# Differential attention in a four-layer trunk: where the heads' splits, the last projection and the first value weights stand in the order of work

## The chip, the cores and the metric

The kernel runs on one core of a Trainium2 chip. The core has five engines, each with its own in-order queue: TensorE (PE in the profile, with its weight loads shown apart as PEld), VectorE (DVE), ScalarE (ACT), GpSimd (POOL) and SyncE (SP), which here only issues loads. The metric is the device time of one execution in microseconds, as the median of several runs. Lower is better.

## The reference

A trunk of four layers over a sequence of 512 positions with 1024 channels, in float32. Layers 0 and 3 mix by a state space (S5), layer 1 by gated linear attention, layer 2 by differential attention; each mixer is followed by a gated feed-forward block. The change touches layer 2's mixer alone:

```python
q, k, v = jnp.split(h @ w_qkv, 3, axis=-1)
q = partial_rope(q.reshape(bsz, seq, 2 * DIFF_HEADS, DIFF_HD), positions) * DIFF_HD ** -0.5
k = partial_rope(k.reshape(bsz, seq, 2 * DIFF_HEADS, DIFF_HD), positions)
v = v.astype(f32).reshape(bsz, seq, DIFF_HEADS, 2 * DIFF_HD)
lam = exp(sum(lam_q1 * lam_k1)) - exp(sum(lam_q2 * lam_k2)) + lambda_init
...
s = jnp.einsum('bqhd,bkhd->bhqk', qb, k)                      # per block of 128 queries
mask = chunk_id[:, None, None, :] <= qcid[:, None, :, None]   # chunks of 64 positions
p = jax.nn.softmax(jnp.where(mask, s, NEG_INF), axis=-1)
a = p[:, :, 0] - lam * p[:, :, 1]
o = jnp.einsum('bhqk,bkhd->bqhd', a, v)
...
o = o * lax.rsqrt(jnp.mean(o * o, axis=-1, keepdims=True) + 1e-5) * subln_g * (1.0 - lambda_init)
x = x + o.reshape(bsz, seq, D_MODEL) @ w_o
```

There are eight heads, each with two score maps of 64 dimensions and values of 128 dimensions.

## The kernel before, in words

**Products.** A float32 product is made of three faster ones. Each operand is split into a high half, a rounded copy made by ACT, and a low half, the difference, made by DVE; `mm3` (L394, matmuls L396 to L398) adds high x high, high x low and low x high into one PSUM accumulator. Weights come in blocks of 256 rows by 512 columns: `wb` (L388) loads a block on SP into one of three staging buffers `wst` (L357) and splits it (L368 on ACT, L376 on DVE) into one of five buffers `whl`.

**Units.** `gemm_units` (L440) is a generator over a projection of 512 output columns: one unit is one `mm3`, for one k tile of 128 rows and one of the four position tiles t, and a projection has 32 units. It asks for a block's load and split just before that block's first unit. At the last k tile each t's accumulator is given to an evacuation function at once.

**Order of the queues.** In this layer the order on PE is the program's own, written by hand. On ACT, DVE, POOL and SP a scheduler that simulates the engines chooses: the ready instruction that comes first in the program goes first, so an instruction can be pulled far ahead of its place when the simulated engine is free, and a queue then runs in the order so fixed. `tc.issue_after(ins)` keeps the instructions made inside it behind `ins` in the order of that engine's queue; it adds no semaphore.

**The layer.** Projections come in the order `project(hf, z)`, half of the heads `hf`, `z` = 0, 1, 2 for q, k, v: the three of half 0, then three of half 1. For q and k the evacuation scales (ACT, L2197) and rotates (DVE, L2202 to L2208) the result, and a `turn` (four PE transposes L2213, one ACT copy L2214 into `qk`) is put into a queue that is due six units later. For v it is one ACT instruction into `vall` (L2219).

`prepare(j)` (L2228) makes head j's operands ready: the split of its q and k (`hl`, ACT L2233, DVE L2234) and eight DMAs on POOL that spread the halves into `qs` (two buffers) and `ks` (in the `whl` buffers). `hl` has one buffer, except for head 1.

The loop has 32 passes, called steps here; step i serves head j = i // 4 and query tile t = i % 4. Its order on PE: `turned(i)`, four transposes of the weighted map `pr` (L2281; ACT copies them to `aT`, L2283); `scores(i + 2)`, four matmuls (L2259) whose softmax (row minimum on DVE L2263, exponential on ACT L2267, combination on DVE L2274) has two steps to finish; `done`, once per head, four transposes of the normalised output (L2314) and its split into `oT` (L516 on ACT, L517 on DVE); some units; `values(i)`, the matmuls with the values (L2291), whose result ACT copies (L2294) and squares (`junk`, L2296); more units. `prepare(j + 1)` stands in the first step of head j. All these transposes and the values share two PSUM banks (`tp`), the scores have two, the projections four.

The units of steps 0 to 14 are those of half 1's projections (`units`, of which ten run ahead of the loop); from step 16 on they are the output projection's first half (`last`), one before and one after the values. The output projection's second half follows the loop with weight blocks `w1` that are asked for at steps 26 and 29. After the layer the feed-forward block runs in a written-out order on all engines.

Of the kernel before, what the change touches and what calls it, by code (L numbers as in the profile page):

```python
# [11 lines left out]
F32 = mybir.dt.float32  # L12
# [3 lines left out]
AF = mybir.ActivationFunctionType  # L16
ALU = mybir.AluOpType
# [5 lines left out]
D = 1024  # L23
SEQ = 512
NT = SEQ // P
KT = D // P
# [262 lines left out]
class Trunk:  # L289
# [147 lines left out]
                    )  # L437
                evac(t, accs[t])

    def gemm_units(self, stat, w, nk, c0, evac):  # L440

        accs = [self.acc() for _ in range(NT)]
        for kb in range(0, nk, 2):
            hl = self.wb(w, kb, c0)
            if kb == 2:
                self.flush()
            for a in range(2):
                k = kb + a
                for t in range(NT):
                    self.mm3(  # L450
                        accs[t][:], stat(k, 0, t), stat(k, 1, t), hl[:, 0, a], hl[:, 1, a], k == 0, k == nk - 1,
                    )
                    if k == nk - 1:
                        evac(t, accs[t])
                    yield
# [1675 lines left out]
    def diff(self, l, left):  # L2131
# [4 lines left out]
        with self.tc.tile_pool(name="diff", bufs=1) as p:  # L2136
# [36 lines left out]
            nc.gpsimd.dma_start(xdv, self.x[:])  # L2173
            vall = []

            queue, clock = [], [0]

            def run(units, n=None):

# [12 lines left out]
            def project(hf, z):  # L2192
                qk = qks[hf]

                def evac(t, ps):
                    q = self.np_.tile([P, 512], F32, tag=("h", "hh")[t % 2], name="qtm", bufs=2)
                    nc.scalar.mul(q[:], ps[:], r[:, t : t + 1])  # L2197
                    s3 = ps[:].rearrange("p (h d) -> p h d", d=64)
                    q3 = q[:].rearrange("p (h d) -> p h d", d=64)
                    ro = p.tile([P, 2, 8, 16], F32, tag="ro", name="ro", bufs=2)  # L2200
                    c2 = cos2[:, t].unsqueeze(1).broadcast_to([P, 8, 16])
                    v.tensor_tensor(ro[:, 0], s3[:, :, 0:16], c2, op=ALU.mult)  # L2202
                    for y in range(2):
                        s1 = sin2[:, t, y * 8 : y * 8 + 8].unsqueeze(1).broadcast_to([P, 8, 8])
                        v.tensor_tensor(  # L2205
                            ro[:, 1, :, y * 8 : y * 8 + 8], s3[:, :, 8 - 8 * y : 16 - 8 * y], s1, op=ALU.mult
                        )
                    v.tensor_tensor(q3[:, :, 0:16], ro[:, 0], ro[:, 1], op=ALU.add)  # L2208

                    def turn():  # L2210
                        tp = self.tp("qTp")
                        for j in range(4):
                            nc.tensor.transpose(tp[:, j], q[:, j * P : (j + 1) * P], self.ident[:])  # L2213
                        nc.scalar.copy(qk[:, z, :, t * P : (t + 1) * P], tp[:])  # L2214

                    queue.append((clock[0] + 6, turn))

                def evac_v(t, ps):
                    nc.scalar.mul(vall[0][:, t, hf * 512 : (hf + 1) * 512], ps[:], r[:, t : t + 1])  # L2219

                if z == 2 and not vall:
                    vall.append(self.xp.tile([P, NT, D], F32, tag="x", name="vall"))
                yield from self.gemm_units(stat, w, KT, z * D + hf * 512, evac_v if z == 2 else evac)

            ready, kept = {}, {}

            def prepare(j):


                room, bufs, tag = (self.wp, 5, "whl") if j == 1 else (p, 1, "hl")  # L2230
                hl = room.tile([P, 2, 2, SEQ], F32R, tag=tag, name="hl", bufs=bufs)
                src = qks[j // 4][:, :, j % 4]
                nc.scalar.copy(hl[:, 0], src)  # L2233
                v.tensor_tensor(hl[:, 1], src, hl[:, 0].bitcast(F32), op=ALU.subtract)  # L2234
                qs = p.tile([P, 2, SEQ], F32R, tag="qs", name="qs", bufs=2)
                ks = self.wp.tile([P, 2, 2, SEQ], F32R, tag="whl", name="ks", bufs=5)
                for m in range(2):
                    rows = slice(m * 64, (m + 1) * 64)
                    for z in range(2):
                        to = slice(z * 64, (z + 1) * 64)  # L2240
                        self.nc.gpsimd.dma_start(qs[to, m], hl[rows, z, 0])
                        self.nc.gpsimd.dma_start(ks[to, m], hl[rows, :, 1])
                ready[j] = qs, ks
                st = self.sp.tile([P, 2, NT], F32, tag="st", name="st", bufs=4)
                o_s = p.tile([P, NT, P], F32, tag="o_s", name="o_s", bufs=2)
                kept[j] = st, o_s
# [3 lines left out]
            def scores(i):  # L2250
                j, t = divmod(i, NT)
                ts = slice(t * P, (t + 1) * P)
                qs, ks = ready[j]
                st = kept[j][0]
                pr, sums = [], self.sp.tile([P, 4], F32, tag="sums", name="sums", bufs=4)
                ss = [self.sbank("s"), self.sbank("s")]
                for m in range(2):
                    for z in range(2):
                        nc.tensor.matmul(ss[m][:], qs[:, m, ts], ks[:, m, z], start=z == 0, stop=z == 1)  # L2259
                for m in range(2):  # L2260
                    e = T("pr", 4)
                    nm = self.sp.tile([P, 1], F32, tag="nm", name="nm", bufs=4)
                    v.tensor_tensor_reduce(  # L2263
                        e[:], ss[m][:], mask[:, t], -0.125, 3e38, op0=ALU.add, op1=ALU.min, accum_out=nm[:]
                    )
                    sum_ = st[:, 0, t : t + 1] if m == 0 else sums[:, 1:2]
                    nc.scalar.activation(e[:], e[:], AF.Exp, scale=-1.0, bias=nm[:], accum_out=sum_)  # L2267
                    pr.append(e)
                v.reciprocal(sums[:, 2:3], sums[:, 1:2])
                v.tensor_scalar(  # L2270
                    sums[:, 3:4], st[:, 0, t : t + 1], sums[:, 2:3], self.neglam[:], op0=ALU.mult, op1=ALU.mult
                )
                a = pr[0]
                v.scalar_tensor_tensor(a[:], pr[1][:], sums[:, 3:4], pr[0][:], op0=ALU.mult, op1=ALU.add)  # L2274
                soft[i] = a
# [24 lines left out]
            def normalised(j):  # L2300
                st, o_s = kept.pop(j)
                q2 = self.sp.tile([P, NT], F32, tag="q2", name="q2", bufs=2)
                v.tensor_tensor(q2[:], st[:, 0], st[:, 0], op=ALU.mult)
                v.scalar_tensor_tensor(q2[:], q2[:], 1e-5, st[:, 1], op0=ALU.mult, op1=ALU.add)
                rs = self.rsqrt(q2[:], NT, 0.0)
                for t in range(NT):
                    v.scalar_tensor_tensor(
                        o_s[:, t], o_s[:, t], rs[:, t : t + 1], sg[:], op0=ALU.mult, op1=ALU.mult
                    )

                def done():
                    tp = self.tp("oTp")
                    for t in range(NT):
                        nc.tensor.transpose(tp[:, t], o_s[:, t], self.ident[:])  # L2314
                    if j == 4:
                        oT[1] = p.tile([P, 2, 4, SEQ], F32, tag="qk", name="oT1", bufs=2)[:].bitcast(F32R)
                    o = oT[j // 4]
                    self.split_t(o[:, 0, j % 4], o[:, 1, j % 4], tp[:].rearrange("p a b -> p (a b)"))

                return done  # L2320

# [33 lines left out]
            run(units, 2)  # L2355
            for i in range(32):
                j, t = divmod(i, NT)
                if i == 15:
                    run(units)
                    rest()  # L2360
                src, n = (units, (3, 3)) if i < 15 else (last, (1, 1))
                if i in (15, 28, 31):
                    n = (0, 0)
                elif i == 29:
                    n = (0, 2)
                aT = turned(i)
                if t == 0 and j < 7:
                    prepare(j + 1)
                if i < 30:
                    scores(i + 2)  # L2370
                if i in done:
                    done.pop(i)()
                run(src, n[0])
                values(i, aT)
                run(src, n[1])
                if i in (16, 31):
                    back(i // 31)
                if i in (26, 29):
                    w1 += [self.wb(wo, kb, 512) for kb in ((0, 2) if i == 26 else (4, 6))]
                if t == 3:  # L2380
                    done[i + (2 if j in (6, 7) else 3)] = normalised(j)
            self.x = vall[0]
# [95 lines left out]
```

## Time and profile before

| | |
|---|---|
| median of three runs | 2300.09 us (2299.6 to 2303.49) |
| the profiled execution | 2300.71 us, span of the core 2298.6 us |
| mean granted TensorE clock | 0.987 |
| instructions | 37231 |
| attention layer, first projection's units to the last output units | about 1166 to 1455 us of the span |
| the loop's 32 groups of four transposes (L2281) | 1248.2 to 1417.2 us |

How to read the rows: a timeline row gives start, length, engine, line, operation, output <- input, and in brackets how long the engine idled before it and what ended that. "PE busy" counts modelled ends, so PE can wait a little less than PEld does. A row of a stretch gives the stretch, its length, the busy time of PE, PEld, DVE, ACT and POOL with their numbers of instructions in brackets, the granted clock, the DMA share and GB/s.

### The profile page before, as it was taken

The numbers are of one execution on the slowest core, as the hardware profiler recorded it, in microseconds if no ns is written. First come the engines' busy times: TensorE is split into PE (matmuls) and PEld (weight loads), VectorE is DVE, ScalarE is ACT, GpSimd is POOL, SyncE is SP. The second block draws the span as 40 slices with busy tenths as digits, with TensorE's granted clock in tenths as the row PEclk, the third lists the DMA queues.
The fourth block names the chain that finished last, engine by engine and source line by source line (L and its number), as shares of the span: only waits on it lengthen the run. The fifth ranks groups of instructions, "written<-read, shape, count | busy, mean of one in ns | idle before, by whom it ended". The sixth has DMA issues, their size and how long they took to land. (4 is left out here: it accounts for less than half of the span.)

```text
span 2298.6 us, 37231 instructions
## 1 busy us (share of the span) xinstructions
PE 2212.9 (96%) x14847; PEld 1961.5 (85%) x14847; DVE 1566.1 (68%) x2430; ACT 1119.9 (49%) x1865; POOL 280.4 (12%) x386
## 2 busy tenths in 40 slices
PE   5889999999999999999999999999999899999997
PEld 3778979898877799998987787989999788989996
DVE  8873887776624469777744675886766964967674
ACT  5534645454452456555535675754534224635342
POOL 1000140512000010101002131110000100101000
PEclk8899999999999999999999999999999999999999
DMA  4136566664422357666336465886641546666521
GB/s 87 39 111 188 139 180 169 171 173 109 121 69 79 123 134 203 183 166 171 98 116 144 95 141 150 214 229 147 163 104 47 143 144 163 176 173 168 159 78 64
DMA packets 295319, 317.83 MB, mean 138 GB/s; under 512 B 72205, under 2 KB 235337, under 8 KB 294890
## 3 DMA queue, kind: packets, MB, share of 16 engines
q1 hardware_dynamic: 232906, 234.23, 33.3%
q0 software_dynamic: 62240, 81.22, 18.9%
q8 instruction: 117, 1.92, 0.3%
q14 instruction: 56, 0.46, 0.1%
HBM read 283.54 MB, written 16.65 MB: 131 GB/s over the span
## 5 line engine op out<-in xcount | busy, mean ns | idle before, releaser
L376 DVE TENSOR_TENSOR whl<-wst,whl 128x1024 fp32r<-128x1024 f32 x272 | 331.1, 1222 | 254.8 <-ACT whl L368 254.2
L368 ACT CAST whl<-wst 128x1024 fp32r<-128x1024 f32 x272 | 284.0, 1050 | 314.7 <-PE acc L398 223.6
L563 PE MATMUL a<-side,whl 128*128 128x256 f32 x3168 | 382.4, 277 | 3.9 <-DVE whl L376 3.6
L563 PEld LDWEIGHTS a<-side,whl 128*128 128x128 f32 x3168 | 369.1, 188 | 6.7 <-DVE whl L376 5.4
L396 PE MATMUL acc<-whl,act 128*128 128x512 f32 x704 | 278.4, 396 | 1.4 <-DVE x L546 1.4
L397 PE MATMUL acc<-whl,act 128*128 128x512 f32 x704 | 274.8, 390 | 0.0
L398 PE MATMUL acc<-whl,act 128*128 128x512 f32 x704 | 274.7, 390 | 0.0
L563 PE MATMUL c<-side,whl 128*128 128x256 f32 x2112 | 254.5, 277 | 1.2 <-DVE whl L376 1.2
L563 PEld LDWEIGHTS c<-side,whl 128*128 128x128 f32 x2112 | 246.8, 188 | 2.0 <-DVE whl L376 2.0
L376 DVE TENSOR_TENSOR whl<-slot,whl 128x1024 fp32r<-128x1024 f32 x107 | 130.4, 1221 | 69.9 <-ACT whl L368 69.9
L396 PEld LDWEIGHTS acc<-whl,act 128*128 128x128 f32 x704 | 132.2, 188 | 31.7 <-issue 2.5
L398 PEld LDWEIGHTS acc<-whl,act 128*128 128x128 f32 x704 | 132.2, 188 | 28.1
L397 PEld LDWEIGHTS acc<-whl,act 128*128 128x128 f32 x704 | 132.2, 188 | 25.6
L368 ACT CAST whl<-slot 128x1024 fp32r<-128x1024 f32 x107 | 112.2, 1053 | 82.3 <-PE acc L398 34.9
L396 PE MATMUL acc<-whl,hT 128*128 128x512 f32 x352 | 144.0, 409 | 2.1 <-DVE ro L2205 1.5
L397 PE MATMUL acc<-whl,hT 128*128 128x512 f32 x352 | 138.9, 395 | 0.9 <-DVE whl L376 0.9
L398 PE MATMUL acc<-whl,hT 128*128 128x512 f32 x352 | 139.2, 395 | 0.0
L563 PE MATMUL a<-sides,whl 128*128 128x256 f32 x1056 | 134.5, 283 | 0.0
L563 PEld LDWEIGHTS a<-sides,whl 128*128 128x128 f32 x1056 | 129.7, 191 | 1.2
L563 PE MATMUL d<-sides,whl 128*128 128x256 f32 x1056 | 126.5, 276 | 1.0 <-ACT whl L368 1.0
L563 PEld LDWEIGHTS d<-sides,whl 128*128 128x128 f32 x1056 | 122.8, 188 | 1.2 <-ACT whl L368 1.2
L702 ACT CAST act<-r 128x512 fp32r<-128x512 f32 (+1 forms) x110 | 66.4, 646 | 114.4 <-DVE r L681 107.3
(452 smaller groups left out, 3891.5 us busy)
## 6 DMA issues: line engine op xcount, KB each, us to landing
wst<-in_ffn_w_gate_up_dram SPq DMA_DIRECT2D x88, 512.0 KB, 4.9
wst<-in_ffn_w_down_dram SPq DMA_DIRECT2D x88, 512.0 KB, 4.1
slot<-in_ffn_w_gate_up_dram SPq DMA_DIRECT2D x71, 512.0 KB, 5.6
wst<-in_ffn_w_gate_up_dram POOLq DMA_DIRECT2D x44, 512.0 KB, 6.0
halves<-in_ffn_w_gate_up_dram SPq DMA_DIRECT2D x43, 512.0 KB, 5.5
wst<-in_s_w_glu_dram SPq DMA_DIRECT2D x32, 512.0 KB, 4.4
wst<-in_gla_w_in_dram SPq DMA_DIRECT2D x24, 512.0 KB, 3.6
wst<-in_diff_w_qkv_dram SPq DMA_DIRECT2D x24, 512.0 KB, 4.0
```

What stands on the lines that cost most here:

```text
L368: self.last["high"] = self.nc.scalar.copy(hl[:, 0], w[:])
L376: self.last["low"] = self.nc.vector.tensor_tensor(hl[:, 1], w[:], hl[:, 0].bitcast(F32), op=ALU.subtract)
L396: mm(out, lh, rh, start=first, stop=False)
L397: mm(out, lh, rl, start=False, stop=False)
L398: self.last["mm"] = mm(out, ll, rh, start=False, stop=last)
L563: mm(o, hl[:, x, k, c], side[y][:, k], start=first and not (j or k or n), stop=k == 3 and n == 2, skip_group_check=True,)
L702: self.last["act high"] = nc.scalar.copy(dst[:, 0, j], src[:, j])
```

## The change

Six edits, all in the layer's order of work; no computation is added or removed.

- `gemm_units` gets `early`: with it, each block's load and split is asked for before the units of the block ahead of it. Only the value projection of half 0 uses it.
- The turns of half 1's q projection are due 6 + t units after their evacuation, so two units apart.
- `prepare(j)`'s ACT copy is tied behind the last evacuation into `vall` made so far (j below 3; none exists yet for j = 0), or behind the last exponential of `scores(4j - 5)` (j from 3).
- Units: at step 3 four units run before the scores and two after the values; steps 9 to 11 take five, steps 12 to 14 four, and step 15 the rest.
- `done` stands at the head of its step, for steps before 29.
- `w1`'s first block is asked for at step 24, the second at 26, and the splits of the two asked for at step 29 are tied behind the copy into `oT`.

```diff
-    def gemm_units(self, stat, w, nk, c0, evac):
+    def gemm_units(self, stat, w, nk, c0, evac, early=False):
         accs = [self.acc() for _ in range(NT)]
+        nxt = None
         for kb in range(0, nk, 2):
-            hl = self.wb(w, kb, c0)
+            hl = nxt or self.wb(w, kb, c0)
+            nxt = self.wb(w, kb + 2, c0) if early and kb + 2 < nk else None
...
-            queue, clock = [], [0]
+            queue, clock, behind = [], [0], {}
...
-                    queue.append((clock[0] + 6, turn))
+                    queue.append((clock[0] + 6 + (t if hf > z else 0), turn))

                 def evac_v(t, ps):
-                    nc.scalar.mul(vall[0][:, t, hf * 512 : (hf + 1) * 512], ps[:], r[:, t : t + 1])
+                    behind["vall"] = nc.scalar.mul(vall[0][:, t, hf * 512 : (hf + 1) * 512], ps[:], r[:, t : t + 1])
...
-                yield from self.gemm_units(stat, w, KT, z * D + hf * 512, evac_v if z == 2 else evac)
+                yield from self.gemm_units(
+                    stat, w, KT, z * D + hf * 512, evac_v if z == 2 else evac, early=z == 2 and not hf
+                )
...
             def prepare(j):
+                tie = behind.get("vall" if j < 3 else 4 * j - 7)
...
-                nc.scalar.copy(hl[:, 0], src)
+                with self.tc.issue_after(tie.ins) if tie else nullcontext():
+                    nc.scalar.copy(hl[:, 0], src)
...
-                    nc.scalar.activation(e[:], e[:], AF.Exp, scale=-1.0, bias=nm[:], accum_out=sum_)
+                    behind[i - 2] = nc.scalar.activation(
+                        e[:], e[:], AF.Exp, scale=-1.0, bias=nm[:], accum_out=sum_
+                    )
...
-                    self.split_t(o[:, 0, j % 4], o[:, 1, j % 4], tp[:].rearrange("p a b -> p (a b)"))
+                    hi = o[:, 0, j % 4]
+                    src = tp[:].rearrange("p a b -> p (a b)")
+                    behind["oT"] = nc.scalar.copy(hi, src)
+                    v.tensor_tensor(o[:, 1, j % 4], src, hi.bitcast(F32), op=ALU.subtract)
...
-                if i == 15:
+                if i == 16:
                     run(units)
                     rest()
-                src, n = (units, (3, 3)) if i < 15 else (last, (1, 1))
-                if i in (15, 28, 31):
+                src, n = (units, (3, 3)) if i < 16 else (last, (1, 1))
+                if i in (28, 31):
                     n = (0, 0)
                 elif i == 29:
                     n = (0, 2)
+                elif 9 <= i < 12:
+                    n = (3, 2)
+                elif 12 <= i < 15:
+                    n = (2, 2)
+                if i in done and i < 29:
+                    done.pop(i)()
                 aT = turned(i)
                 if t == 0 and j < 7:
                     prepare(j + 1)
+                if i == 3:
+                    run(src, 4)
+                    n = (0, 2)
                 if i < 30:
                     scores(i + 2)
                 if i in done:
...
-                if i in (26, 29):
-                    w1 += [self.wb(wo, kb, 512) for kb in ((0, 2) if i == 26 else (4, 6))]
+                for kb in {24: (0,), 26: (2,), 29: (4, 6)}.get(i, ()):
+                    self.behind = {"silu": behind["oT"], "scaled": behind["oT"]} if i == 29 else None
+                    w1.append(self.wb(wo, kb, 512))
+                    self.behind = None
```

`self.behind` is what `high` and `low` (L365, L371) read to put a split behind the named instructions.

## Prediction

> **What bounds the kernel now.** I read the page's busy shares first, then a table of stretches through the attention layer, then what the weight loads (PEld) wait for there, and last the timeline around each of those waits.
>
> ```profile
> PE 2212.9 (96%) x14847; PEld 1961.5 (85%) x14847; DVE 1566.1 (68%) x2430; ACT 1119.9 (49%) x1865; POOL 280.4 (12%) x386
> ```
>
> TensorE bounds the whole, at 96%. No edit changes the matmuls, so only PE's idle time inside this layer can be won. Stretches of the layer (length, then busy PE, PEld, DVE, ACT and POOL with instruction counts, clock, DMA):
>
> ```profile
> 1170.00:1240.00 70.00, 68.44 (x312) 56.01 (x310) 24.77 (x56) 24.55 (x33) 6.89 (x12) 0.98 0.49 137
> 1270.00:1290.00 20.00, 17.18 (x98) 13.94 (x97) 13.02 (x42) 14.01 (x32) 4.34 (x5) 1.00 0.14 38
> 1320.00:1350.00 30.00, 29.98 (x166) 25.36 (x164) 18.34 (x46) 18.77 (x46) 10.06 (x17) 1.00 0.66 141
> 1350.00:1380.00 30.00, 27.89 (x169) 23.56 (x170) 26.11 (x71) 24.80 (x70) 12.23 (x19) 1.00 0.63 134
> 1380.00:1421.00 41.00, 35.38 (x206) 27.88 (x205) 27.52 (x75) 26.15 (x77) 4.13 (x4) 1.00 0.37 96
> 1421.00:1455.00 34.00, 34.00 (x197) 29.44 (x197) 16.94 (x24) 20.92 (x57) 5.74 (x5) 1.00 0.85 209
> ```
>
> PE idles at four places: before 1240 (1.6 us, with a clock below 1), at 1270 to 1290 (2.8), and 2.1 and 5.6 us in the two stretches from 1350 on, where softmaxes run with few projection units between them. Around these PE is full. What PEld waited for between 1170 and 1421 (total us, times, longest):
>
> ```profile
> PEld op L2291 <- ACT aT L2283: 5.5, 7, 1.5
> PEld acc L396 <- ACT oT L516: 2.8, 2, 1.9
> PEld acc L396 <- ACT qtm L2197: 1.9, 1, 1.9
> PEld acc L398 <- DVE oT L517: 1.4, 2, 1.0
> PEld op L2291 <- ACT qk L2214: 1.4, 1, 1.4
> PEld oTp L2314 <- ACT junk L2296: 1.4, 2, 1.1
> PEld acc L397 <- DVE whl L376: 1.3, 1, 1.3
> PEld aTp L2281 <- DVE oT L517: 1.2, 1, 1.2
> PEld acc L396 <- ACT whl L368: 1.1, 1, 1.1
> PEld s L2259 <- DVE nm L2263: 1.0, 2, 0.6
> PEld aTp L2281 <- ACT junk L2296: 0.7, 1, 0.7
> ```
>
> These are 19.7 us, nearly all on copies made by ACT and DVE, not on DMA or PE. PEld counts also the gap that PE's pipeline covers, so I take a little less than each row.
>
> **Part 1: the value projection's weights a step ahead.**
>
> ```profile
> 1218.42 1.05 ACT L2233 CAST hl<-qk 128x1024 fp32r<-128x1024 f32 x1
> 1219.38 2.93 ACT L368 CAST whl<-wst 128x1024 fp32r<-128x1024 f32 x3
> 1220.47 0.19 PEld L396 LDWEIGHTS acc<-whl,hT 128*128 128x128 f32 x1 [1.05 <-ACT whl L368]
> 1221.92 0.19 PEld L397 LDWEIGHTS acc<-whl,hT 128*128 128x128 f32 x1 [1.26 <-DVE whl L376]
> 1219.47:1222.89 3.42, 1.86 (x7) 1.04 (x6) 3.38 (x3) 2.84 (x4) 2.75 (x5) 1.00 0.54 104
> 1222.89:1226.30 3.41, 3.41 (x9) 2.66 (x9) 1.25 (x2) 0.00 (x0) 1.80 (x4) 0.50 1.00 230
> ```
>
> The second weight block of the value projection is split only after head 0's split, because the program asks for it after `prepare(0)`. PE waits 1.05 us for its high half and 1.26 for its low half. In the next 3.41 us the clock is 0.50, and half of 3.41 is 1.7. With `early`, the block is asked for before the first eight units, where ACT has nothing to do, so its split is done when PE comes. Later blocks are asked for a block ahead, and a block, 24 matmuls at the 68.44 us for 312 of the first stretch, is 5.3 us of PE, longer than the two splits in front of it (2 x 1.05 on ACT). Three loads of 512 KB (blocks two to four) move earlier on SP with it, past nothing: that queue holds only weight loads, and the stretch before 1219 has little DMA. Bounds: nothing (the block still comes late) to 2.3 + 1.7 = 4.0. I take 2.1 + 1.6 = **3.7 saved**.
>
> [...]
>
> **Part 2: heads' splits tied to later points, first unit group at step 3, turns apart.** (Step i is a pass of the loop.)
>
> ```profile
> 1269.67 1.05 ACT L2233 CAST hl<-qk 128x1024 fp32r<-128x1024 f32 x1 [3.48 <-DMA ks<-hl]
> 1274.55 0.19 PEld L396 LDWEIGHTS acc<-whl,hT 128*128 128x128 f32 x1 [1.88 <-ACT qtm L2197]
> 1282.58 0.97 PEld L2291 LDWEIGHTS op<-vall,aT 128*128 128x128 f32 x8 [1.42 <-ACT qk L2214]
> 1370.34 1.05 ACT L2233 CAST hl<-qk 128x1024 fp32r<-128x1024 f32 x1 [1.52 <-DMA ks<-hl]
> 1371.30 0.58 ACT L2283 COPY aT<-aTp 128x512 f32<-128x512 f32 x1
> 1371.92 0.97 PEld L2291 LDWEIGHTS op<-vall,aT 128*128 128x128 f32 x8 [1.51 <-ACT aT L2283]
> ```
>
> A head's split stands on ACT ahead of its use and waits there for the previous head's copies to leave `hl`; the aT copy that PE needs is queued behind it, at step 3 and at step 20. Tied two steps later, the buffer is free and the split doesn't block.
>
> - Step 20: of 1.51 I take **1.4 saved**.
> - Step 3: the four last units of the q projection now come before the scores, with scores and values (the 1.18 and 0.97 of the rows here and below) between them and the first unit that reuses their accumulators. The 1.88 goes, and the aT wait beside it (part of the 5.5): **2.3 saved**. DVE takes the rotation ahead of the row minima, so the next scores may wait for their bank; I leave 0.2 for that.
> - Step 4: the values waited 1.42 for the third turn's bank. With two units between turns a copy like aT's 0.58 fits, unless it stands behind two exponentials (0.72 each, row below): **0.9 saved**.
>
> What the ties cost: they are an order on ACT's queue, not a semaphore; heads 1 and 2 go behind the value evacuations (four of the 0.69 of the first row below) and are needed two steps and more later, so nothing. The 1.05 us copies of heads 5, 6 and 7 still come, in other steps; the bounds are 0 and 1.05 each, and I take 0.3 each since ACT has gaps (24.80 of 30 busy): **0.9 lost**. Behind the split are eight DMAs on POOL:
>
> ```profile
> L2219 ACT ACTIVATE vall<-acc,rcol x8: 682/690/690, 1237.9 to 1350.0; 128x512 f32<-128x512 f32 x8
> 1372.91 1.22 DVE L2234 TENSOR_TENSOR hl<-qk,hl 128x1024 fp32r<-128x1024 f32 x1
> 1377.39 0.72 ACT L2267 ACTIVATE pr<-pr,nm 128x512 f32<-128x512 f32 x1
> 1393.90 1.18 PE L2259 MATMUL s<-ks,qs 128*128 128x512 f32 x4
> DMA to landing us min/median/max: 3.2/6.1/9.8
> ```
>
> Head 7's tie is the exponential that ends near 1378.3 (third row, with its read of the sum); its first scores are the fourth row. Copy 1.05, low half 1.22 (second row) and eight issues, estimated at 0.6 each from POOL's 4.34 busy in x5 and 12.23 in x19 instructions (0.64 to 0.87, the pow among them), end near 1385.4; a landing (last row, `ks`, 1368 to 1392) at the median gives 1391.5, at the maximum 1395.2, against 1393.9 less what the earlier savings pull it forward, some 1.7. So head 7 ranges from 0.7 early to 3.0 late, head 6 about the same. POOL's rsqrt for the head before is queued behind those issues. I take **1.0 lost** for the two; the bounds are 0 and 2 x (3.0 + 1.6 of clock).
>
> **Part 3: the value projection through step 15, `done` first, output splits tied.**
>
> ```profile
> 1351.03 0.42 PEld L2281 LDWEIGHTS aTp<-ident,pr 128*128 128x128 f32 x4 [1.25 <-DVE oT L517]
> 1397.49 0.19 PEld L398 LDWEIGHTS acc<-whl,oT 128*128 128x128 f32 x1 [1.00 <-DVE oT L517]
> 1409.12 1.05 ACT L368 CAST whl<-wst 128x1024 fp32r<-128x1024 f32 x1
> 1411.48 0.57 ACT L516 CAST oT<-oTp 128x512 fp32r<-128x512 f32 x1
> ```
>
> Of the 96 units 10 run ahead of the loop. Before, steps 0 to 13 took six each (84), step 14 the last two and step 15 none. Now 9 x 6 + 3 x 5 + 3 x 4 + 5 = 86 reach through step 15, out of steps where PE is full (29.98 of 30) into steps where it waits. Step 15's wait of 1.25 and part of the aT waits go, since five units are there to run meanwhile: **1.2 saved**. The four value evacuations now end just before step 16's values need them: 0 to 2 x 0.69, I take **0.4 lost**.
>
> At step 26 the head's output is split and used in one step (0.91 and 1.00, within the oT rows 2.8 and 1.4). With `done` first there are transposes and scores between: **1.2 saved** of 1.9. At step 29 a weight split of 1.05 stands ahead of the oT copy; the tie puts it behind: **1.9 saved** of 2.3. The tied splits of blocks 4 and 6 are needed only after step 31, when PE has full work from the blocks before; SP's next loads, which wait for their staging buffers, move by some 2 us into a stretch where PE is full. In exchange aT's transposes now take the PSUM bank of the last step's values, right after them, at steps 18, 22 and 26. The nearest rows are the waits on junk, 1.4 for two and 0.7 for one; with bounds of 0 and 1.1 I take 0.5 each: **1.5 lost**. The output block asked for at step 24 instead of 26 costs nothing: it spreads two loads on SP and two splits over four steps, and takes one of five buffers two steps sooner (two hold keys, one the current block).
>
> **The sum.** Saved 3.7 + 1.4 + 2.3 + 0.9 + 1.2 + 1.2 + 1.9 = 12.6; lost 0.9 + 1.0 + 0.4 + 1.5 = 3.8; net 8.8. The profiled execution took 2300.71 (span 2298.6, 2.1 around it), 0.6 above the median of 2300.09. So 2300.7 - 8.8 = 2291.9, or 2291.3 as a median; I say 2291.5. The layer after is full of PE work (34.00 of 34) and starts as much earlier, its first loads having room.
>
> **The rivals.**
> - *No new waits*: gains whole, costs nil. 2300.1 - 13.6 - 1.7 = 2285. For it: ACT and DVE are at most 87% busy from 1350 on. Against: an in-order queue stalls locally.
> - *The softmax end gives it back*: the four terms from step 14 on (5.7) are eaten by bank order and ACT's new order. 2300.1 - 6.9 + 3.8 = 2297, no change by measure. For it: DVE 26.11 and ACT 24.80 of 30 there.
> - *The early block isn't early*: its buffer isn't free, since the same pool holds heads' keys. 2291.5 + 3.7 = 2295.2. Against: ACT and DVE are idle before it.
> - *The clock drop stays* by itself after part 1: 2293.
> - *Slower: the keys of heads 5 to 7 land late.* Place: their first scores. The longest landing of `ks`, in the stretch 1218 to 1245, is:
>
> ```profile
> DMA to landing us min/median/max: 3.3/4.8/11.7
> ```
>
> With 11.7 head 7 is 1385.4 + 11.7 - 1392.2 = 4.9 late, and such a stall in a window of 3.41 brings the half clock of part 1 (1.6): 6.5 each, 19 for three, against 9.8 net without this term: 2300.1 - 9.8 + 19 = 2309. It makes the kernel slower by more than 0.2% once the three cost over 4.8 each. Against: the median is half of that, head 5 has more time (its steps hold five units), and `qs` couldn't be refilled sooner before either: scores read its old buffer until that point.
>
> **How the numbers follow.** Forecast 0.53 (its own range 2287 to 2295), no new waits 0.10, softmax end 0.17, not early 0.07, clock stays 0.04, slower 0.09. A median of this kernel tells 0.2% or 4.6 us: faster is below 2295.5. Half of "not early" counts as faster: 0.53 + 0.10 + 0.04 + 0.03 = 0.70; same 0.17 + 0.04 = 0.21; slower 0.09. The range 2285 to 2298 leaves out the slower case and the tails.
>
> **What would show it.** Part 1: no wait near 1220 and a clock of 1.00 there. Part 2: hl rows without a DMA wait, no qtm wait, no qk wait above 0.5. Part 3: oT waits below 1.5 in sum; junk waits grown to some 3. The prediction is wrong if scores wait for DMA at steps 18, 22 and 26, or if the stretch from step 16 on isn't shorter by some 3 us.

## The result, and the profile after

The changed kernel took 2291.28 us as the median of 6 runs (2286.95 to 2294.17) beside 2303.5 for the kernel before (6 runs, 2299.6 to 2305.39). The ratio is 0.9947, interval 0.9937 to 0.9957: 12.2 us shorter, 9.9 to 14.5. The forecast was 2291.5, 8.6 us below the 2300.1 known then. That the time itself came out within 0.3 us is luck: in these runs the kernel before stood 3.4 higher, and the saving was 3.6 larger.

The profiled execution took 2286.95 us, 13.8 less than the one before. Part of that isn't the change's, and the layer's own length tells it apart. The layer's first load and the first transposes of its output, in the timelines of the kernel before and of the changed kernel:

```profile
1166.28 0.34 SPq L2147 DMA_DIRECT2D kb<-in_positions_dram  x1
1434.67 0.60 PE L123 MATMUL tp<-ident,vall 128*128 128x128 f32 x4
```

```profile
1162.97 0.34 SPq L2149 DMA_DIRECT2D kb<-in_positions_dram  x1
1421.04 0.60 PE L123 MATMUL tp<-ident,vall 128*128 128x128 f32 x4
```

From first to last row the layer took 268.39 us before and 258.07 after: **10.3 us less**. Another 3.3 were gained ahead of the layer, in code that the change doesn't touch; behind it the two are alike (863.9 and 864.2 us to the end of the span). The page's granted clocks show it in the first two of 40 slices, the kernel before first:

```profile
PEclk8899999999999999999999999999999999999999
```

```profile
PEclk9999999999999999999999999999999999999999
```

A second profile of the changed kernel (the last experiment) has 8 in those slices too and began the layer at 1170.58, later than before. So the layer's own length is the measure below, and whole times carry a few us of this spread.

The page's busy shares:

```profile
PE 2207.4 (97%) x14847; PEld 1959.2 (86%) x14847; DVE 1566.8 (69%) x2430; ACT 1121.4 (49%) x1865; POOL 281.7 (12%) x386
```

The stretches that answer to those of before (length, busy PE, PEld, DVE, ACT, POOL with counts, clock, DMA):

```profile
1166.69:1236.69 70.00, 70.00 (x328) 58.05 (x327) 24.53 (x58) 26.39 (x34) 7.06 (x12) 1.00 0.49 138
1262.95:1283.00 20.05, 20.05 (x118) 17.32 (x117) 14.67 (x45) 14.43 (x35) 4.01 (x5) 1.00 0.24 66
1310.00:1340.00 30.00, 30.00 (x168) 25.64 (x167) 22.07 (x55) 20.30 (x53) 10.07 (x17) 1.00 0.75 151
1337.00:1367.00 30.00, 29.58 (x177) 25.32 (x175) 23.27 (x65) 24.43 (x67) 8.48 (x13) 1.00 0.56 138
1367.00:1408.00 41.00, 35.44 (x210) 28.83 (x209) 29.97 (x80) 28.08 (x79) 8.04 (x11) 1.00 0.47 117
1408.00:1442.00 34.00, 34.00 (x201) 29.53 (x200) 16.89 (x24) 21.55 (x57) 5.64 (x5) 1.00 0.84 213
```

The first two of the four idle places are gone, and the clock of the first is 1.00. The third fell from 2.1 to 0.4 us idle. The fourth is as empty as before: 5.56 of 41 us idle. What PEld waited for in the layer:

```profile
PEld acc L398 <- DVE oT L2329: 2.3, 2, 1.2
PEld op L2299 <- ACT aT L2291: 2.1, 5, 1.0
PEld s L2265 <- DVE nm L2269: 2.0, 2, 1.7
PEld aTp L2289 <- ACT junk L2304: 1.9, 2, 1.2
PEld acc L396 <- ACT oT L2328: 1.1, 1, 1.1
PEld aTp L2289 <- ACT qk L2216: 0.5, 1, 0.5
PEld aTp L2289 <- issue: 0.4, 2, 0.2
```

The sum fell from 19.7 to 10.3 us, and no wait on a DMA is among them. The whl and qtm rows are gone; the oT rows (3.4) and junk (1.9) stay.

A step is the time from its first weight load of `aTp` to the next step's. "Ahead" is the stretch from half 0's first k turn to the first scores. In us, all from starts in the timelines:

| | ahead | step 3 | step 4 | 9 to 16 | step 20 | 25, 26 | 28, 29 | layer |
|---|---|---|---|---|---|---|---|---|
| before | 27.35 | 9.08 | 9.06 | 45.70 | 5.00 | 10.22 | 10.81 | 268.39 |
| changed | 23.60 | 6.91 | 7.71 | 44.55 | 3.54 | 9.79 | 10.53 | 258.07 |
| early blocks alone | 24.87 | 7.57 | 9.07 | 45.69 | 5.29 | 10.22 | 11.27 | 266.00 |
| early at mid-block | 25.32 | 8.02 | 9.04 | 45.66 | 4.61 | 10.21 | 10.81 | 265.37 |
| early, heads 1 and 2 tied | 23.59 | 9.32 | 9.05 | 45.68 | 4.69 | 10.20 | 11.31 | 266.16 |
| ties alone | 25.74 | 7.29 | 8.85 | 45.77 | 3.65 | 9.90 | 10.85 | 263.56 |
| changed, done late | 23.60 | 6.94 | 7.73 | 44.17 | 3.66 | 11.07 | 10.20 | 258.72 |
| changed, units as before | 23.59 | 6.94 | 7.73 | 45.43 | 3.46 | 9.06 | 10.56 | 259.10 |
| changed, turns together | 23.60 | 6.95 | 9.21 | 44.55 | 3.52 | 9.36 | 10.53 | 259.35 |
| changed, step 3 as before | 23.60 | 7.29 | 7.73 | 44.55 | 3.55 | 9.05 | 10.68 | 259.03 |
| changed, done first at 29 | 23.59 | 6.94 | 7.73 | 44.54 | 3.52 | 8.84 | 9.03 | 256.16 |
| changed, split tied at 26 | 23.59 | 6.94 | 7.73 | 44.54 | 3.52 | 8.11 | 10.47 | 256.55 |
| both of these | 23.60 | 6.94 | 7.74 | 44.55 | 3.52 | 8.10 | 8.93 | 255.48 |
| changed, second profile | 23.60 | 6.94 | 7.74 | 44.55 | 3.52 | 9.07 | 10.62 | 258.68 |

Half clocks within the layer (a granted clock of 0.50) are part of these times: one ahead of the scores in the kernel before, and one at steps 29 and 30 (some 1.2 us) in both kernels with early blocks, without and with the tie, in those with units or step 3 as before, and in the second profile.

### The profile page after: what moved, and what is told of

The parts are those of the page before. It is cut to its first block, busy times and chain, and to the rows that moved or that the text cites. A ratio compares the mean times of both kernels' runs of the same rounds, so it can differ in the third digit from the quotient of the medians.

```text
span 2285.2 us, 37227 instructions
## 1 busy us (share of the span) xinstructions
PE 2207.4 (97%) x14847; PEld 1959.2 (86%) x14847; DVE 1566.8 (69%) x2430; ACT 1121.4 (49%) x1865; POOL 281.7 (12%) x386
## 4 chain that ended last, share of the span: by engine, by line
PE 81%; DVE 9%; ACT 4%; issue 3%; DMA 2%; SPq 1%; POOL 0%; ACTq 0%; DVEq 0%; POOLq 0%
PE a L565 18%; PE acc L396 13%; PE acc L398 13%; PE acc L397 13%; PE c L565 8%; PE d L565 4%; PE y L1474 2%; DVE whl L376 2%; ACT whl L368 1%; PE V L1438 1%; PE s L2265 1%; PE op L2299 1%; PE tp L123 1%; DVE halves L229 1%; ACT halves L211 1%
## 5 line engine op out<-in xcount | busy, mean ns | idle before, releaser
L396 PE MATMUL acc<-whl,hT 128*128 128x512 f32 x352 | 141.8, 403 | 0.0
L398 PE MATMUL acc<-whl,hT 128*128 128x512 f32 x352 | 137.5, 391 | 0.0
L397 PE MATMUL acc<-whl,hT 128*128 128x512 f32 x352 | 137.3, 390 | 0.0
```

The source lines that it names most:

```text
L396: mm(out, lh, rh, start=first, stop=False)
L397: mm(out, lh, rl, start=False, stop=False)
L398: self.last["mm"] = mm(out, ll, rh, start=False, stop=last)
```

## The experiments

The diffs are shortened to the lines that matter; a shortened line is marked by dots or a comment.

### The early blocks, alone and with a tie

```diff
+ def gemm_units(..., early=False):        # to the kernel before
+     hl = nxt or self.wb(w, kb, c0)
+     nxt = self.wb(w, kb + 2, c0) if early and kb + 2 < nk else None
```

> The kernel before, with the early weight block alone. Theory (the wait and the half clock behind it are one cost): the stretch from the first turn of half 0's k projection to the first scores falls from 27.35 us to about 23.6 as in the changed kernel, the granted clock stays 1.00 there, everything from the first scores to the end of the layer (1241.1 to 1434.7, 193.5 us) stays within 0.5 us, and the time falls by some 3.7 us. Rival (the half clock has another cause and stays): the stretch falls by 2.1 only, with a 0.50 clock left in it.

Measured: 2301.56 against 2304.71 us, ratio 0.9991 (0.9981 to 1.0001), so the times don't show a gain for certain. The wait for the second block and the clock drop after it are gone (1.00 from 1214.35 to 1243.35), but only 2.5 of 3.75 us are won: another wait has come, on a value evacuation. From the first scores on it took 193.63 us, within 0.5 as forecast, but by offsetting: step 3 was 1.5 shorter, and a half clock made steps 28 to 30 1.3 longer. The timeline of this kernel:

```profile
1236.77 1.05 ACT L2235 CAST hl<-qk 128x1024 fp32r<-128x1024 f32 x1 [3.63 <-DMA ks<-hl]
1237.72 2.42 ACT L2221 ACTIVATE vall<-acc,rcol 128x512 f32<-128x512 f32 x4
1238.45 0.19 PEld L396 LDWEIGHTS acc<-whl,hT 128*128 128x128 f32 x1 [1.40 <-ACT vall L2221]
```

A head's split stands on ACT for 3.63 us, waiting for `hl` to come free, with the evacuations behind it. The tie of heads 1 and 2 puts it behind them:

```diff
+ behind["vall"] = nc.scalar.mul(vall[0]...)      # on top of the early blocks
+ tie = behind.get("vall") if j < 3 else None
```

> The kernel before with the early blocks and the tie of heads 1 and 2 behind the value evacuations, nothing else. With the early blocks alone the stretch from the last turn to the first scores took 24.87 us against 23.60 in the changed kernel, with a new wait of 1.40 for an evacuation, behind which heads' splits stood. If that tie, priced at nothing in the prediction, is what the early blocks need: the wait goes and the stretch is 23.5 to 23.8. Rival (something else of the change does it): a wait near 1.4 remains and the stretch is 24.7 to 25.0.

The first theory held: 23.59, and a stretch without a gap or a drop:

```profile
1216.00:1245.00 29.00, 29.00 (x137) 24.05 (x136) 11.19 (x21) 15.39 (x21) 7.57 (x14) 1.00 0.69 143
```

So part 1's 3.75 us take both edits. The layer is only 2.2 shorter, since steps 29 and 30 lost 1.3 us to a half clock, and the whole time (2302.13 in one run, beside 2302.03) doesn't show it. Asking for the next block at the middle of a block instead,

```diff
+ if early and k == 1 and t == NT - 1: nxt = self.wb(w, kb + 2, c0)
```

> The kernel before, with the second weight block of half 0's value projection asked for after the eighth unit, that is late, but ahead of head 0's split. PE should still wait, about 0.2 us for the high half and 0.9 for the low half, 1.1 instead of 2.3. Theory (the clock halves when a window of 3.41 us has too little PE work, the limit being somewhere near the 1.86 us of the window before the drop): about 2.5 us of work in the window, no drop, the stretch from the first turn to the first scores at about 24.8 us. Rival (the drop isn't tied to the amount of waiting): a 0.50 clock again, about 26.4 us.

gave 2296.32 us in one run, 25.32 ahead of the scores and the same kind of wait (1.85 for an evacuation). PE didn't wait for the block at all, so the waits of 0.2 and 0.9 us on which this was to try the clock didn't come, and how much waiting brings the drop is not shown by it.

### The ties alone

```diff
+ tie = behind.get("vall" if j < 3 else 4 * j - 7)      # to the kernel before
+ with self.tc.issue_after(tie.ins) if tie else nullcontext():
```

> The kernel before, with the ties of the heads' splits alone. Theory (a split pulled far ahead waits at the head of ACT's queue for the last head's DMAs, and aT behind it): the waits of ACT for ks<-hl (10.4 us in 4) go, step 20 falls from 5.00 to about 3.6 us, step 3 from 9.08 to about 8 (the accumulator wait of 1.9 stays), and from the first step to the last the layer is 2.3 to 3.0 us shorter. Rival (the split only moves and delays aT elsewhere): step 20 falls, but steps 13, 17 and 21, where it lands, grow by 0.5 to 1.0 each, and the sum is under 1 us shorter. A second rival (late keys): scores wait for DMA at steps 18, 22 or 26.

Measured: 2299.48 us, the layer 4.8 shorter. From the first scores on it was 190.31 instead of 193.54. Step 3 won 1.8 by the tie alone and step 20 1.35. Neither rival came: steps 13, 17 and 21 stayed within 0.03 us of before (22 and 26 grew by 0.3 each), and no scores waited for a DMA. The value weights came as late as before, yet the clock stayed at 1.00 and the stretch ahead was 1.6 shorter (25.74 instead of 27.35), which is the drop's price (see the end).

### Step 3's units, and the turns

```diff
- if i == 3: run(src, 4); n = (0, 2)
```

> The changed kernel with step 3's units where they were, three ahead of the values and the rest behind. It tests whether the 2.2 us won at step 3 come from moving these units, as the prediction had it (a wait of 1.88 for the rotated copies qtm), or from the tie of the head's split. With the ties alone step 3 took 7.29 and the wait was 0.48. If the move makes it: step 3 takes 8.5 us or more here. If the tie makes it: 7.1 to 7.5 against 6.91, so the move is worth only some 0.4 us, and the layer is 0.2 to 0.6 longer.

Step 3 took 7.29, just what the ties alone gave, with the wait for `qtm` at 0.48. Moving the units is worth 0.36; the tie made the rest.

```diff
- queue.append((clock[0] + 6 + (t if hf > z else 0), turn))
+ queue.append((clock[0] + 6, turn))
```

> The changed kernel with the turns due as before, all of one projection at once. It tests the term of 0.9 for step 4, which measured 1.35 in the changed kernel (9.06 to 7.71). If the spacing of the turns makes it: the values' wait of about 1.4 us for a turn's bank is back, step 4 takes 8.9 us or more, and the layer is 1.2 to 1.5 us longer than 258.07. Rival (the head's split, that no longer blocks ACT, makes it): step 4 stays within 0.4 of 7.71.

Step 4 took 9.21, with the wait back. The spacing is worth 1.5 there, and 1.7 over steps 0 to 8.

```profile
1275.89 0.97 PEld L2299 LDWEIGHTS op<-vall,aT 128*128 128x128 f32 x8 [1.59 <-ACT qk L2216]
```

### The value projection's units, and done at its old place

```diff
- if i == 16: run(units); rest()      # and the counts of steps 9 to 14
+ if i == 15: run(units); rest()
```

> The changed kernel with the value projection's units spread as before: six a step through step 13, the last two at step 14, none at step 15. It tests the term of 1.2 us for steps 14 and 15 less 0.4 for the late evacuation at step 16. If the spread is what gains there: a wait of about 1 us comes back at step 15 (bank held by oT), steps 9 to 16 take 45.2 to 45.7 us against 44.55. If the earlier ties made the gain, and the spread only moves work: steps 9 to 16 stay within 0.3 us of 44.55. Either way the part from step 17 on shouldn't move.

Steps 9 to 16 took 45.43: the spread is worth 0.9. The wait that came back was one for aT, not for oT:

```profile
1348.57 0.97 PEld L2299 LDWEIGHTS op<-vall,aT 128*128 128x128 f32 x8 [1.26 <-ACT aT L2291]
```

```diff
- if i in done and i < 29: done.pop(i)()
```

> The changed kernel with the head's output transposes (done) back behind the scores. Theory (done first gives the oT split time at step 26, and costs waits on junk for the shared bank): oT waits at step 26 grow from 1.1 to about 1.9 us, junk waits fall from 1.9 to about 1, steps 14 to 27 change by less than 0.7 us in sum. Rival (done first was the gain at the softmax end): steps 14 to 27 get longer by 1.5 us or more.

The layer was 258.72, 0.65 more than in the first profile of the changed kernel. Steps 9 to 16 were 0.4 shorter and junk's waits went, but steps 25 and 26 took 11.07 with scores waiting 2.41 us behind DVE's `sums` and 0.91 for oT. Steps 14 to 27 took 60.40 instead of 58.49, 1.9 longer, where the theory allowed 0.7: that is the rival's sign, though some 0.55 of it are the transposes of step 14, which stood ahead of that step's start when they came first. So done first is worth 1.3 to 2.0 at steps 25 and 26 (against 9.79 and 9.07 in the two profiles of the changed kernel), and its cost in bank order is real. Over the layer 0.65 is left against the first profile, and nothing against the second (258.68), which has a half clock of some 1.2 in it.

### What held the end back: steps 26 and 29

The changed kernel's timeline at step 29 (PEld, PE and ACT rows):

```profile
1394.02 0.30 PEld L2265 LDWEIGHTS s<-ks,qs 128*128 128x128 f32 x2 [1.65 <-DVE nm L2269]
1394.72 0.71 ACT L2273 ACTIVATE pr<-pr,nm 128x512 f32<-128x512 f32 x1
1395.20 0.60 PE L2322 MATMUL oTp<-ident,o_s 128*128 128x128 f32 x4
1395.59 0.72 ACT L2273 ACTIVATE pr<-pr,nm 128x512 f32<-128x512 f32 x1
1396.31 0.71 ACT L2273 ACTIVATE pr<-pr,nm 128x512 f32<-128x512 f32 x1
1397.01 0.56 ACT L2328 CAST oT<-oTp 128x512 fp32r<-128x512 f32 x1
1397.62 0.19 PEld L396 LDWEIGHTS acc<-whl,oT 128*128 128x128 f32 x1 [1.12 <-ACT oT L2328]
1399.17 0.19 PEld L398 LDWEIGHTS acc<-whl,oT 128*128 128x128 f32 x1 [1.25 <-DVE oT L2329]
```

The transposes end at 1395.80, and the weight split is indeed behind the copy (at 1397.90), but the copy waits behind exponentials. The waits for the two halves of oT, 2.4 us, are what they were in the kernel before (1.86 and 0.43). There, two exponentials stood between the weight split (1409.12, in the prediction) and the copy (1411.48):

```profile
1410.06 0.73 ACT L2267 ACTIVATE pr<-pr,nm 128x512 f32<-128x512 f32 x1
1410.78 0.71 ACT L2267 ACTIVATE pr<-pr,nm 128x512 f32<-128x512 f32 x1
```

```diff
- if i in done and i < 29:
+ if i in done and i < 30:
```

> The changed kernel with the finished heads' output done first at step 29 too. It tests the term that failed, step 29. Changed kernel: oTp is done at 1395.6, but ACT makes the copy oT only at 1397.01, behind three exponentials, and PE waits 1.12 and 1.25 us for the two halves; steps 28 and 29 took 10.53 us. Theory (the copy's place on ACT's queue is the cause, not the weight split that the tie moved): with the output first the copy stands ahead of the exponentials, the two waits fall below 0.5 each, and steps 28 to 30 are 1.5 to 2 us shorter, layer 256 to 256.6 against 258.07. Rival (normalising is the cause): the head's output isn't normalised when step 29 begins, so PE waits some 1.4 us at the transposes oTp instead and the layer stays within 0.5 us of 258.07.

Time 2291.01 us, ratio 0.9947 (0.993 to 0.9963). Both oT waits of step 29 are gone; a part of the rival came true:

```profile
1399.15 0.86 PEld L2322 LDWEIGHTS oTp<-ident,o_s 128*128 128x128 f32 x4 [0.74 <-PE op L2299]
1402.77 0.97 PEld L2299 LDWEIGHTS op<-vall,aT 128*128 128x128 f32 x8 [1.37 <-ACT aT L2291]
```

Steps 28 to 30 took 12.55 instead of 13.56: 1.0 won, not 1.5 to 2. The rest of the layer's 1.9 was won at step 25, which this edit doesn't touch: there ACT stands in front of a weight split until its load lands, and that varied. The changed kernel, then this one:

```profile
1379.18 1.05 ACT L368 CAST whl<-wst 128x1024 fp32r<-128x1024 f32 x1 [1.71 <-DMA wst<-in_diff_w_o_dram]
1381.41 0.42 PEld L2289 LDWEIGHTS aTp<-ident,pr 128*128 128x128 f32 x4 [1.23 <-ACT junk L2304]
```

```profile
1385.62 1.04 ACT L368 CAST whl<-wst 128x1024 fp32r<-128x1024 f32 x1 [0.74 <-DMA wst<-in_diff_w_o_dram]
1387.86 0.42 PEld L2289 LDWEIGHTS aTp<-ident,pr 128*128 128x128 f32 x4 [0.23 <-ACT junk L2304]
```

```diff
- self.behind = {...} if i == 29 else None
+ self.behind = {...} if i in (26, 29) else None
```

> The changed kernel with the splits of the output block that is asked for at step 26 tied behind the copy oT, as those asked for at step 29 are. It tests why step 26 gained 0.4 us and not 0.7. Changed kernel: ACT stands 1.71 us at 1379.18 in front of a weight split whose load hasn't landed, with exponentials queued behind it; PE then waits 1.23 for a bank (junk) and 1.08 for oT; steps 25 and 26 take 9.79 us. Theory: the split's load is the cause, and with the tie steps 25 to 27 are 1 to 2 us shorter, layer 256 to 257. Rival: the split comes later but then stands right ahead of the aT copy of step 26 or 27 (1.05 us), and the layer stays within 0.5 us of 258.07.

2288.48 us in one run. No ACT row in these steps waits for a weight load any more, and the wait of 1.08 for oT is gone. Steps 25 to 27 took 11.95 instead of 13.44, or of 12.48 where the load landed sooner: 0.5 to 1.5 won.

Both edits together:

```diff
- if i in done and i < 29:
+ if i in done and i < 30:
- self.behind = {...} if i == 29 else None
+ self.behind = {...} if i in (26, 29) else None
```

> The changed kernel with both edits: output done first at step 29 too, and the splits asked for at step 26 tied behind oT. If the two causes (copy behind exponentials at step 29; split waiting for its load at step 26) are separate, the gains add: layer 254.5 to 256 against 258.07, and some 2 to 3.5 us off the changed kernel's time. If both only move the wait, the layer is within 0.7 us of 258.07 and the time the same.

2288.03 us (6 runs, 2282.64 to 2290.47), ratio 0.9934 (0.992 to 0.9947): the shortest layer of all. It is 255.48, 2.6 under the changed kernel's. The two gains add: 1.1 at steps 28 to 30 and 1.5 at steps 25 to 27, against the first profile. The interval of the ratio overlaps with the changed kernel's, so the trace shows the gain while the times lean the same way. What PEld mainly waits for in it:

```profile
PEld op L2299 <- ACT aT L2291: 4.0, 6, 1.4
PEld aTp L2289 <- ACT junk L2304: 1.1, 2, 0.7
PEld oTp L2322 <- PE op L2299: 0.8, 1, 0.8
```

### The changed kernel again, without an edit

> The changed kernel once more, without an edit. Its first profile lost 1.71 us on ACT at step 26 to a load that hadn't landed; the kernel with the output done first at step 29, which is the same up to there, lost 0.74. If the landing varies from run to run: steps 25 and 26 take 8.8 to 9.8 us here, and the layer is 257 to 258.1; all other steps agree with the first profile within 0.1. The ratio to before should lie in 0.9937 to 0.9957 again.

2292.0 us (6 runs) against 2302.03, ratio 0.9949 (0.993 to 0.9967). Steps 25 and 26 took 9.07, with a wait of 0.97 for the load: its landing does vary. The miss is step 30, 4.26 instead of 3.03, by a half clock, and with it the layer: 258.68 instead of 257 to 258.1.

## Why the prediction was right, point by point

The total held: 8.8 forecast within the layer, 10.3 and 9.7 measured in two profiles. The terms were not all right, and part of the closeness is luck, as errors of opposite sign offset.

- **Part 1** (3.7): 3.75. But the tie of heads 1 and 2, priced at "nothing" because those heads are needed late, carries 1.3 of it. I asked when the split is needed and not what stands behind it on ACT. And 1.6 of the 3.75 is the half clock of the one profile of the kernel before, the same that the prediction read; where the late weights cost no half clock, 2.1 are left (25.74 against 23.60).
- **Step 3** (2.3): 2.2, by the wrong cause. The prediction gave the 1.88 to the units' move; the tie makes 1.8 and the move 0.36.
- **Step 4** (0.9): 1.35, of the spacing as said. Step 20 (1.4): 1.46, of the tie as said.
- **Steps 14, 15 and the late evacuation** (1.2 - 0.4): 1.15 over steps 9 to 16, 0.9 of it the spread's.
- **Step 26 and the bank order** (1.2 - 1.5): steps 25 and 26 won 0.4 to 1.2. Junk's waits were 1.9 and 1.2 in the two profiles, against 2.1 on aTp and oTp before, not 3. The load in front of ACT was in no term. No run asks for the block of step 24 at its old place alone, so that this "costs nothing" isn't shown.
- **Step 29** (1.9): **the failed step**, 0.3. "The tie puts it behind" is true of the split. But the split takes 1.05, so its leaving could win no more than that; 1.9 was booked as if the copy then ran at once. The copy met the next obstacle on the same queue, three exponentials, and the scores ahead of the transposes waited 1.65 (0.64 before) for the row minima (`nm`) to free their bank. The prediction didn't ask what is late next, and the two exponentials of the kernel before stood in its own timeline.
- **Late keys** (-1.0) **and moved copies** (-0.9): no scores wait for a DMA, and the aT waits, where a copy in the way would show, fell from 5.5 to 2.1. The tie did put head 7's split behind the exponential that it names: in the changed kernel this ended at 1364.8, and the split began at 1364.96 (forecast for 1378.3 of the old timeline, which is 13.4 later; 3.3 of them come from ahead of the layer). The last of its `ks` issues began at 1370.3 (issue 0.64, longest landing 8.8 in that stretch), so the keys were there by 1379.7 at the latest, and the scores came at 1381.83.

Three of the stated signs failed. The oT waits are 3.4 instead of below 1.5, mostly by step 29 (2.4). Junk's waits didn't grow to 3. And from step 16 on the layer is 1.7 us shorter (1.76 from step 17, none at 16) instead of some 3, which the prediction had named as a sign that it is wrong. Its own terms don't give 3 there either: 1.4 + 1.2 + 1.9 saved, less 0.6 for the copies of heads 6 and 7, 1.0, 0.4 and 1.5, make 1.0. The saving at step 29 was 1.6 too high; of the 3.4 booked for keys, copies and bank order the waits show little. Those are the errors that offset.

## What to carry to other kernels

On an in-order queue, price a moved instruction by what stands behind it, not by when its result is needed: the split that waited 3.63 us for its buffer held up the value evacuations behind it, and PE waited 1.40 us for one of them. And when a blocker is taken away, look up the next one in the same queue before booking the gain: at step 29 exponentials and a bank took the split's place, and 1.6 of the 1.9 us weren't won. Compare a layer by its own two ends; the layer of one and the same kernel began 7.6 us apart in two profiles.

## What the runs showed of the clock

The same wait was followed by a half clock in one execution and not in another: behind the late value weights the granted clock was 0.50 in the kernel before and 1.00 in the kernel with the ties alone. In the traces of the kernel before and of the changed kernel all changes of the clock lie multiples of 3.41 us apart (658 times 3.413 from 41.88 to 2287.84 us, and 653 times from 46.97 to 2275.88). Stretches of that length, each with the one that follows, of the kernel with the ties alone, of the second profile of the changed kernel, of the early blocks alone and of the early blocks at mid-block:

```profile
1221.36:1224.78 3.42, 2.04 (x8) 1.12 (x6) 2.23 (x2) 3.39 (x5) 1.59 (x3) 1.00 0.21 41
1224.78:1228.19 3.41, 3.22 (x14) 2.69 (x15) 2.40 (x3) 0.57 (x1) 2.96 (x6) 1.00 0.91 175
```

```profile
1403.40:1406.81 3.41, 1.67 (x8) 0.95 (x7) 3.30 (x8) 3.41 (x8) 0.00 (x0) 1.00 0.01 2
1406.81:1410.23 3.42, 3.42 (x14) 2.78 (x13) 1.50 (x2) 0.60 (x2) 0.00 (x0) 0.50 0.47 127
```

```profile
1407.27:1410.68 3.41, 1.74 (x10) 1.12 (x10) 3.41 (x9) 2.83 (x9) 0.00 (x0) 1.00 0.94 292
1410.68:1414.09 3.41, 3.41 (x11) 2.65 (x11) 0.36 (x1) 0.59 (x1) 0.00 (x0) 0.50 0.05 16
```

```profile
1404.61:1408.02 3.41, 1.74 (x14) 1.40 (x12) 3.41 (x11) 3.41 (x10) 0.00 (x0) 1.00 0.76 220
1408.02:1411.43 3.41, 3.38 (x19) 2.34 (x18) 0.95 (x2) 0.59 (x1) 0.00 (x0) 1.00 0.25 90
```

Stretches with 1.86 (in the prediction), 1.74 and 1.67 us of PE work were followed by 0.50; the one with 2.04 wasn't, and neither was another with 1.74. So the busy time of the profile doesn't separate these rows. It goes by modelled ends: a matmul of 512 columns counts 0.39 us, though the next one follows after 0.226. An estimate from the starts does separate the stretches of this layer in three profiles, of the kernel before and the two of the changed kernel: with 0.226 us for a matmul of 512 columns and 0.109 for one of 128, their spacings back to back in these traces, the two stretches that a half clock followed hold 1.29 us (kernel before) and 1.1 (second profile of the changed kernel), and no other holds less than 1.5.

The waits alone didn't decide it. The first and the second profile have the same waits at step 29 to within 0.02 us (scores 1.65 and 1.67, the halves of oT 1.12 and 1.13, 1.25 and 1.24). In the first they are spread over two stretches (1.99 and 2.20 us busy, with a clock of 1.00 behind both), in the second one stretch holds 1.67, 0.50 followed, and the second lost 1.3 us more over steps 29 and 30. The 1.6 us of part 1 are thus a price that the profile of the kernel before paid and that of the ties alone, with the late weights kept, didn't. PE was busy for 1.67 us or more in each of the three stretches that 0.50 followed.
